# Attention steps of two heads and two key blocks, and rotary temporaries taken off the pooling chain, in a fused decoder block on eight cores

## Chip, cores, metric

One Trainium2 chip, all 8 NeuronCores, each with two of the 16 sequences (4096 tokens). The metric is the time of the slowest core, in microseconds (us), as the median of several executions. "Before" was 1694 us (1692 to 1696, 3 runs).

Executions come in two states. In the slow state the cores of one or both dies show a lower granted TensorE clock and the run is some per cent longer. One core has TensorE (PE), with its weight loads shown apart (PEld), VectorE (DVE), ScalarE (ACT), GpSimd (POOL) and the sync queue (SP), which here issues only DMAs.

## The reference, cut to what matters

```python
h   = x + concat[ MLA(n), POOL(n) ] @ w_out        # n = rmsnorm(x)
h   = h + relu(rmsnorm(h) @ w_up)**2 @ w_down
out = rmsnorm(h)

# MLA: latents c_q (384), c_kv (256), shared rotary key k_rope (64); 4 heads of 128 + 64 rotary
s = einsum(q, k) * scale                  # causal
o = softmax(s) @ v
# POOL: 4 channel groups, trailing means over 2, 4, 8, 16 tokens, minus the token itself
pooled = (cs - lo) / cnt - x
```

SEQ is 2048, D_MODEL 1024, D_FF 4096. Everything is float32 at the interface; the kernel's matmuls run in bf16.

## The kernel before

A tile is 512 tokens; a core has 8 tiles, four per sequence. Attention of tile t is one long loop over head pairs and key blocks. Into it the kernel weaves "filler" chunks: the output projection of tile t-1 (W), then all input projections of tile t+1 (P), then the transposes for tile t+2 (N). The feed-forward part comes after all eight tiles.

PSUM has 8 banks of 128x512 float32. During attention, three are fixed (two output accumulators, one for the row sums), and five rotate first-in first-out among the scores and the filler:

```python
bank = deque(range(8)); OB = (5, 6); RB = 7        # 5, 6, 7 leave the queue when attention begins
def acquire(): return bank.popleft()
def release(k): bank.append(k)
```

One attention step before: one key block j, two heads a. The rotary part of the score has 64 rows, the rest 128.

```python
def emit_S(i):
    pr, j = steps[i]
    ks = [acquire(), acquire()]
    for a, k in enumerate(ks):
        r = slice(64 * a, 64 * a + 64)
        mm(pm[k], kpe[sl][r, o:o + P], qpe[qs][r, pr, q0:T], True, False, ...)      # 64-row shape
    for a, k in enumerate(ks):
        mm(pm[k], knT[sl][:, h, o:o + P], qn[qs][:, h, q0:T], False, True, ...)     # full shape
    for k in ks:
        act(pT[p], pm[k], AF.Exp, ...); release(k)
        # diagonal blocks: masked by VectorE
# per step: emit_S(i + 1); filler; then P.V of step i (full), and after every second j
# four row-sum matmuls (32-column shape)
```

The pooled sums run on POOL, as one chain over the four groups with two temporaries, sA and sB. The rotary query of the second head pair uses the same two:

```python
def u_group(g):
    k = win_mm(768 + g * P, "win_b")
    act(u[:, 16:16 + T], pm[k], AF.Copy, ...)                       # the chain starts here
    for l in range(1, g + 2):
        dst = sA if l % 2 == 1 else sB
        tt("pool", dst[...], src[...], src[...], ALU.add, ...)
    # ... scale, subtract, write the pooled half of mixT

def q_rope(pr):
    tmp = (rstd[:, 0, :], rstd[:, 1, :]) if pr == 0 else (sA[:, 0:T], sB[:, 0:T])
    for w in range(2):
        # 3 matmuls into a bank
        tt("dve", tmp[w], pm[k], cs[:, w, :], ALU.mult, ...)
    tt("dve", qpe[qs][:, pr, :], tmp[0], tmp[1], ALU.add, ...)
```

The output projection needs x again. It has two buffers for four row blocks, so the load of block 2 waits until the store of block 0 has landed:

```python
def f(b, nh, part):                                   # W, row block b
    # 8 matmuls
    tt("dve", d, pm[k], d, ALU.add, ...)              # d: half of xr[b % 2]
    if nh == 1:
        dma("sp", rows(out_d, t, b), xr[b % 2], ...)  # store
        if b + 2 < 4: ld(b + 2)                       # load x into the same buffer
```

And POOL's queue also issues the conversion of the feed-forward weights from float32 to bf16, HBM to HBM, in 16 pieces. They depend on nothing, so they go out when POOL is through with the chain that stands ahead of them in its queue (at 217.3 us in the timeline below):

```python
STAGE = [...]                                          # 8 pieces of w_up, 8 of w_down
def stage(n):
    for _ in range(min(n, len(STAGE))):
        dma("pool", o, i, (), [r])
# "g": two calls inside P, one inside the next tile's W
```

The softmax here doesn't subtract the row's maximum and nothing guards it: scores larger than these inputs give would overflow.

## Time and profile before

The profile records one execution. First, of the kernel before, the head of its page: the span and PE's busy time with its share.

```profile
span 1682.4 us, 23203 instructions; the slowest of 8 cores (1672.6 to 1682.4 us)
## 1 busy us (share of the span) xinstructions
PE 1503.3 (89%) x7484; PEld 661.2 (39%) x7484; DVE 581.9 (35%) x873; ACT 597.4 (36%) x1147; POOL 366.1 (22%) x387
```

The table of stretches for the kernel before, on its slowest core: attention, then feed-forward (the start is left out). Columns are length, busy time of PE, weight loads, VectorE, ScalarE and POOL with counts, granted clock, DMA share, GB/s.

```profile
78.30:765.00 686.70, 554.87 (x2922) 223.90 (x2922) 262.27 (x454) 320.07 (x629) 191.06 (x207) 0.92 0.48 112
765.00:1682.40 917.40, 909.84 (x4373) 418.78 (x4373) 275.16 (x352) 239.29 (x454) 141.59 (x128) 1.00 0.13 48
```

PE fills the feed-forward stretch (910 of 917 us). In the attention stretch it is idle for 132 of 687 us. Why is in the list of waits of the kernel before (who <- for whom: us in total, times, longest). L323 is the matmul helper, L332 the two-operand elementwise helper; "arena" is all of SBUF, so the names say little and the engines much.

```profile
PE pm L323 <- DVE arena L332: 134.8, 32, 14.2
DVE arena L332 <- DMA arena<-x: 83.5, 11, 14.7
DVE arena L332 <- POOL arena L332: 82.7, 8, 14.1
PE pm L323 <- ACT arena L329: 2.1, 5, 0.5
```

PE waits for VectorE, and VectorE for two things: eight times (once per tile) for POOL, and for loads of x. Both can be seen in one tile's timeline (kernel before, end of tile 1 and start of tile 2; start, length, engine, line, operation, and in brackets the idle time before it and what ended it):

```profile
204.34 1.62 PE L323 MATMUL pm<-arena 128*128 128x512 bf16 x10
...
216.13 1.26 POOL L332 TENSOR_TENSOR arena<-arena 128x512 bf16<-128x512 f32 x1
217.33 1.57 POOL L353 DMA_DIRECT2D wup_bf<-w_mlp_up  x3
217.49 1.29 DVE L332 TENSOR_TENSOR arena<-pm,arena 128x512 f32<-128x512 f32 x2 [12.89 <-POOL arena L332]
218.33 0.59 PE L323 MATMUL pm<-arena 64*128 64x128 bf16 x3 [12.37 <-DVE arena L332]
...
218.92 0.33 SPq L353 DMA_DIRECT2D arena<-cs_tab  x1
...
239.23 0.36 SPq L353 DMA_DIRECT2D out<-arena  x1
...
253.85 0.35 SPq L353 DMA_DIRECT2D arena<-x  x1
...
258.44 0.69 DVE L332 TENSOR_TENSOR arena<-pm,arena 128x512 f32<-128x512 f32 x1 [14.66 <-DMA arena<-x]
259.27 1.12 PE L323 MATMUL pm<-arena 64*128 64x512 bf16 x2 [8.85 <-DVE arena L332]
```

At 217.3 POOL ends its chain. VectorE, which has waited 12.9 us for sA, goes on, and so does PE. At the same moment POOL issues three weight conversions, and 1.6 us later the loads of the cosine table (cs_tab) follow, which had waited for VectorE. At 239.2 the store of row block 0 goes out; the load that waits for it is issued only at 253.9, 14.6 us later (a store's median is 3.1 us), and PE stands another 8.9 us.

What a change of shape costs PE can be read from the start times of its matmuls: 216 ns from one full 128x512 matmul to the next, 312 ns from a full one to a 64-row pair, 319 ns from the pair back to a full one. So each change costs about 0.1 us.

### The profile page before, as it was taken

What the parts mean: (1) busy time and instruction counts of PE and PEld (TensorE: products, weight loads), DVE (VectorE), ACT (ScalarE), POOL (GpSimd) and SP (SyncE); (2) the same over time, 40 slices, a digit from 0 to 9 for tenths busy, and PEclk for the clock granted to TensorE, in tenths of its full rate; (3) what the DMA queues carried; (4) which work ended last, traced back from release to release, by engine and by line L of the source; (5) the groups of instructions that cost most, each with busy time, mean ns of one, the idle gap of its engine ahead of it and who ended that gap; (6) DMA issues with size and microseconds to landing.
All of it is one profiled execution on the core that took longest, in us unless ns stands there. A gap on an engine that the chain in (4) does not pass through costs nothing.

```text
span 1682.4 us, 23203 instructions; the slowest of 8 cores (1672.6 to 1682.4 us)
## 1 busy us (share of the span) xinstructions
PE 1503.3 (89%) x7484; PEld 661.2 (39%) x7484; DVE 581.9 (35%) x873; ACT 597.4 (36%) x1147; POOL 366.1 (22%) x387
## 2 busy tenths in 40 slices
PE   5567878788867879799999999999999999999998
PEld 2223333333322333233444444444444444444443
DVE  5543524314352524233332331333323313333222
ACT  6354535445332535462224123232241232322312
POOL 1650411406060513301111111110121112101210
PEclk9799988999988989999999999999999999999999
DMA  9344272643837171375402011020020110200001
GB/s 297 103 133 109 99 100 72 128 108 88 150 88 129 47 125 64 139 224 173 165 26 76 0 51 51 1 101 1 23 79 0 49 53 1 101 1 19 32 1 51
DMA packets 36133, 137.08 MB, mean 81 GB/s; under 512 B 4272, under 2 KB 4272, under 8 KB 35120
## 3 DMA queue, kind: packets, MB, share of 16 engines
q1 hardware_dynamic: 31616, 105.66, 18.8%
q0 software_dynamic: 4064, 29.36, 10.5%
q8 instruction: 64, 1.05, 0.3%
q10 hardware_dynamic: 336, 0.57, 0.1%
q14 instruction: 53, 0.43, 0.1%
HBM read 118.28 MB, written 51.38 MB: 101 GB/s over the span
## 4 chain that ended last, share of the span: by engine, by line
PE 75%; POOL 11%; DMA 6%; ACT 3%; issue 3%; DVE 2%; POOLq 0%; DVEq 0%; ACTq 0%; SPq 0%
PE pm L323 73%; POOL arena L332 8%; DMA out<-arena 4%; POOL arena L338 3%; ACT arena L329 2%; DMA arena<-x 2%; PE pm L326 2%; DVE arena L332 1%; POOL arena L347 1%; DVE arena L341 0%; DVE arena L347 0%; POOL arena L353 0%; ACT arena L390 0%; POOLq L125 0%; DVEq L125 0%
## 5 line engine op out<-in xcount | busy, mean ns | idle before, releaser
L323 PE MATMUL pm<-arena 128*128 128x512 bf16 (+3 forms) x6968 | 1472.1, 379 | 141.1 <-DVE arena L332 134.8
L323 PEld LDWEIGHTS pm<-arena 128*128 128x128 bf16 (+3 forms) x6968 | 626.2, 98 | 972.4 <-issue 303.0
L329 ACT ACTIVATE arena<-pm 128x512 bf16<-128x512 f32 (+4 forms) x768 | 412.0, 569 | 845.8 <-PE pm L323 770.6
L332 POOL TENSOR_TENSOR arena<-arena 128x512 bf16<-128x512 f32 (+6 forms) x248 | 280.6, 1131 | 776.1 <-ACT arena L329 755.6
L332 DVE TENSOR_TENSOR arena<-pm,arena 128x512 f32<-128x512 f32 (+2 forms) x288 | 197.5, 690 | 594.4 <-PE pm L323 372.4
L332 DVE TENSOR_TENSOR arena<-arena 128x512 bf16<-128x512 f32 (+3 forms) x355 | 195.0, 564 | 385.7 <-ACT arena L329 382.9
L329 ACT ACTIVATE arena<-arena 128x1 f32<-128x1 f32 (+5 forms) x200 | 104.6, 530 | 209.9 <-DVE arena L332 191.0
L335 DVE SCALAR_TENSOR_TENSOR arena<-arena 128x1024 bf16<-128x1024 f32 (+1 forms) x64 | 82.6, 1319 | 66.5 <-ACT arena L329 66.5
L347 POOL COPY arena<-arena 128x16 f32<-128x16 f32 x48 | 14.6, 304 | 338.0 <-ACT arena L329 338.0
L390 ACT ACTIVATE arena<-arena 128x1024 bf16<-128x1024 f32 x64 | 67.7, 1057 | 16.5 <-DMA arena<-out 11.6
L326 PE MATMUL pm<-arena 128*128 128x128 bf16 x516 | 41.0, 236 | 30.5 <-DVE arena L341 27.4
L326 PEld LDWEIGHTS pm<-arena 128*128 128x128 bf16 x516 | 36.1, 107 | 40.8 <-issue 35.5
L338 POOL TENSOR_SCALAR arena<-arena 128x512 f32<-128x512 f32 x32 | 49.0, 1530 | 2.6 <-POOL arena L332 1.3
L347 DVE COPY arena<-pm 128x1024 bf16<-128x1024 bf16 (+1 forms) x65 | 42.2, 681 | 18.5 <-PE pm L326 18.4
L341 DVE TENSOR_SCALAR arena<-arena 128x1024 bf16<-128x1024 f32 (+4 forms) x48 | 43.2, 912 | 12.4 <-ACT arena L329 7.4
L347 DVE CAST arena<-pm 128x512 bf16<-128x512 f32 x40 | 25.6, 685 | 17.0 <-PE pm L323 16.9
L350 POOL MEMSET arena<- 128x16 f32 (+3 forms) x15 | 2.4, 172 | 71.0 <-ACT arena L329 70.6
L353 POOL DMA_DIRECT2D arena<-wup_bf x8 | 5.7, 707 | 50.0 <-DMA arena<-wup_bf 50.0
L390 ACT ACTIVATION_READ_ACCUMULATOR arena<-arena 128x1 f32 x64 | 12.5, 195 | 0.0
L353 POOL DMA_DIRECT2D arena<-arena x8 | 4.7, 590 | 35.7 <-ACT arena L329 35.7
L329 ACT ACTIVATE arena<-pm,arena 128x512 f32<-128x512 f32 x16 | 10.9, 680 | 1.0 <-PE pm L323 0.9
L329 ACT ACTIVATION_READ_ACCUMULATOR arena<-arena 128x1 f32 x32 | 6.0, 186 | 0.0
(17 smaller groups left out, 22.9 us busy)
## 6 DMA issues: line engine op xcount, KB each, us to landing
arena<-x SPq DMA_DIRECT2D x64, 512.0 KB, 4.6
out<-arena SPq DMA_DIRECT2D x64, 512.0 KB, 3.1
arena<-out SPq DMA_DIRECT2D x28, 512.0 KB, 5.7
wup_bf<-w_mlp_up POOLq DMA_DIRECT2D x8, 1024.0 KB, 18.8
wdn_bf<-w_mlp_down POOLq DMA_DIRECT2D x8, 1024.0 KB, 24.0
arena<-wup_bf POOLq DMA_DIRECT2D x8, 1024.0 KB, 7.6
arena<-wdn_bf SPq DMA_DIRECT2D x8, 1024.0 KB, 16.8
arena<-cs_tab SPq DMA_DIRECT2D x28, 128.0 KB, 28.3
```

Source lines behind the costliest of these rows:

```text
L323: return S.add("pe", lambda e: e.matmul(out, lhsT=lhsT, rhs=rhs, start=start, stop=stop, skip_group_check=skip), reads, writes)
L326: return S.add("pe", lambda e: e.transpose(out=out, in_=in_, identity=ident), list(reads) + ["ident"], writes)
L329: return S.add("act", lambda e: e.activation(out=out, in_=in_, func=func, **kw), reads, writes, extra=extra)
L332: return S.add(eng, lambda e: e.tensor_tensor(out=out, in0=in0, in1=in1, op=op), reads, writes, extra=extra)
L335: return S.add(eng, lambda e: e.scalar_tensor_tensor(out=out, in0=in0, scalar=scalar, in1=in1, op0=op0, op1=op1), reads, writes, extra=extra)
L338: return S.add(eng, lambda e: e.tensor_scalar(out=out, in0=in0, scalar1=s1, scalar2=s2, op0=op0, op1=op1), reads, writes)
L341: return S.add(eng, lambda e: e.tensor_scalar_mul(out, in0, s1), reads, writes)
L347: return S.add(eng, lambda e: e.tensor_copy(out=out, in_=in_), reads, writes)
L350: return S.add(eng, lambda e: e.memset(ap, val), (), writes)
L353: return S.add(eng, lambda e: e.dma_start(out=out, in_=in_), reads, writes, dma=True, extra=extra)
L390: S.add("act", lambda e: e.activation(out=ring[b % len(ring)][0], in_=xs[:, b, :], func=AF.Square, scale=1.0 / 32.0, accum_out=ss_t[:, so ...
```

## The change

Its intent: (1) steps of two key blocks, so that four 64-row, four full and four row-sum matmuls each stand together and PE changes shape less often; (2) both rotary pairs use rstd as temporary, so VectorE no longer waits for POOL; (3) the cosine load leaves W; (4) at the start, rotary angles first and weight scaling split between ScalarE and VectorE. The diff, cut to its core:

```diff
         def q_rope(pr):
-            tmp = (rstd[:, 0, :], rstd[:, 1, :]) if pr == 0 else (sA[:, 0:T], sB[:, 0:T])
-            nm = [("rstd", 0), ("rstd", 1)] if pr == 0 else ["sA", "sB"]
+            nm = [("rstd", 0), ("rstd", 1)]
...
-                tt("dve", tmp[w], pm[k], cs[:, w, :], ALU.mult, [("pm", k)] + CSN, [nm[w]])
+                tt("dve", rstd[:, w, :], pm[k], cs[:, w, :], ALU.mult, [("pm", k)] + CSN, [nm[w]])
...
-        steps = [(pr, j) for pr in range(2) for j in range(nkb)]
+        steps = [(pr, j) for pr in range(2) for j in range(0, nkb, 2)]
...
-            ks = [acquire(), acquire()]
-            for a, k in enumerate(ks):
+            bl = [(j, a, max(0, j - 4 * c) * P, acquire()) for j in (j0, j0 + 1) for a in range(2)]
+            for j, a, q0, k in bl:
                 r = slice(64 * a, 64 * a + 64)
                 mm(pm[k][:, 0:T - q0], kpe[sl][r, o:o + P], qpe[qs][r, pr, q0:T], True, False,
...   # likewise the full matmuls, the exponentials, P.V and the row sums, four at a time
-    rope_angles()
     for kc in range(8):
-        win_scale(winb_f, "win_b", 640, kc, "act")
+        win_scale(winb_f, "win_b", 640, kc, ("act", "dve")[kc % 2])
...
     for j in range(3):
-        tsm("dve", wq[:, j, 0:768], wq_f[:, j, 0:768], gq_c[:, j:j + 1], ["wq_f", "sm"], ["wq"])
         tsm("dve", halves(wq, j, 0), halves(wq_f, j, 0), gqn_t[:, j:j + 1], ["wq_f", "gqn"], ["wq"])
         tsm("dve", halves(wq, j, 1), halves(wq_f, j, 1), gq_c[:, j:j + 1], ["wq_f", "sm"], ["wq"])
+        act(wq[:, j, 0:768], wq_f[:, j, 0:768], AF.Copy, ["wq_f", "sm"], ["wq"], scale=gq_c[:, j:j + 1])
...
+    P_chunks(1)["cs"][1]()
...   # cut: position loads on the sync queue, the cosine chunk moved behind the transposes
```

More of the change, by code (lines that the diff above doesn't have):

```diff
@@ L360, in build_program @@
     for q in range(4):
-        dma("act", posi[q * 32:(q + 1) * 32, :], pos_d[q * D:(q + 1) * D].partition_broadcast(32), (), [("posi", q)])
+        dma("sp", posi[q * 32:(q + 1) * 32, :], pos_d[q * D:(q + 1) * D].partition_broadcast(32), (), [("posi", q)])
     for b in range(4):
@@ L538, in q_rope @@
                     mm(pm[k], wq[:, j, c0:c0 + P], sq[:, j, :], j == 0, j == 2, ["wq", ("sq", j)], [("pm", k)])
-                tt("dve", tmp[w], pm[k], cs[:, w, :], ALU.mult, [("pm", k)] + CSN, [nm[w]])
+                tt("dve", rstd[:, w, :], pm[k], cs[:, w, :], ALU.mult, [("pm", k)] + CSN, [nm[w]])
                 release(k)
-            tt("dve", qpe[qs][:, pr, :], tmp[0], tmp[1], ALU.add, nm, [("qpe", qs, pr)])
+            tt("dve", qpe[qs][:, pr, :], rstd[:, 0, :], rstd[:, 1, :], ALU.add, nm, [("qpe", qs, pr)])
         def qn_group(h):
@@ L581, in P_chunks @@
         return d
-    FLOW = ("cs c0 c1 n0 c2 n1 c3 n2 c4 n3 kr sq nr fs u3 sk s0 u2 kp s1 u1 s2 u0 g r0 q0 t0 q1 r1 t1 q2 t2 q3 t3 "
+    FLOW = ("c0 c1 n0 c2 n1 c3 n2 c4 n3 kr sq nr fs u3 sk s0 u2 kp s1 u1 s2 u0 g r0 q0 t0 q1 r1 t1 q2 t2 q3 t3 cs "
             "k0 k1 k2 k3 v0 v1 v2 v3 g").split()
@@ L660, in emit_S @@
         def emit_S(i):
-            pr, j = steps[i]
-            sl, o = (t0 + j // 4) % KVS, (j % 4) * P
-            q0 = max(0, j - 4 * c) * P
-            ks = [acquire(), acquire()]
-            for a, k in enumerate(ks):
+            pr, j0 = steps[i]
+            bl = [(j, a, max(0, j - 4 * c) * P, acquire()) for j in (j0, j0 + 1) for a in range(2)]
+            for j, a, q0, k in bl:
+                sl, o = (t0 + j // 4) % KVS, (j % 4) * P
                 r = slice(64 * a, 64 * a + 64)
@@ L668, in emit_S @@
                    [("kpe", sl), ("qpe", qs, pr)], [("pm", k)])
-            for a, k in enumerate(ks):
+            for j, a, q0, k in bl:
+                sl, o = (t0 + j // 4) % KVS, (j % 4) * P
                 h = 2 * pr + a
@@ L672, in emit_S @@
                    [("knT", sl, h), ("qn", qs, h)], [("pm", k)])
-            ps = []
-            for k in ks:
+            out = []
+            for j, a, q0, k in bl:
                 p = pti[0]
@@ L680, in emit_S @@
                     tt("dve", pT[p][:, 0:P], pT[p][:, 0:P], keep, ALU.min, [("pT", p), "keep"], [("pT", p)])
-                ps.append(p)
-            live[i] = (j, q0, sl, ps)
+                out.append((j, a, q0, (t0 + j // 4) % KVS, p))
+            live[i] = out
         def fin1():
@@ L702, in attention @@
         for i in range(n):
-            pr, j = steps[i]
+            pr, j0 = steps[i]
             if i + 1 < n:
                 emit_S(i + 1)
-            if j == 0 and pr == 1:
+            if j0 == 0 and pr == 1:
                 fill(max(total * i / n, done[0] + 6))
                 run_late()
-            fill(max(total * (i + 1) / n, done[0] + (20 if j == 0 else 0)))
-            j, q0, sl, ps = live[i]
-            for a in range(2):
+            fill(max(total * (i + 1) / n, done[0] + (22 if j0 == 0 else 0)))
+            bl = live.pop(i)
+            for j, a, q0, sl, p in bl:
                 h = 2 * pr + a
-                mm(pm[OB[a]][:, q0:T], Vc[sl][:, j % 4, h * P:(h + 1) * P], pT[ps[a]][:, 0:T - q0], j == 0, j == nkb - 1,
-                   [("V", sl, j % 4), ("pT", ps[a])], [("O", a)])
-            if j % 2 == 1:
-                for jj, qq, _, pp in (live[i - 1], live[i]):
-                    for a in range(2):
-                        if c > 0:
-                            qd, w = 64 * a + 32 * (jj % 2), 32
-                            st, sp = jj < 2, jj >= nkb - 2
-                        else:
-                            qd, w = 64 * a, 64
-                            st, sp = jj == 0, jj == nkb - 1
-                        mm(pm[RB][qd:qd + w, qq:T], ones[:, 0:w], pT[pp[a]][:, 0:T - qq], st, sp, ["ones", ("pT", pp[a])], ["R"], skip=True)
-                del live[i - 1], live[i]
-                if j + 1 == nkb:
-                    fin1()
-                    late.append(lambda pr=pr: fin2(pr))
+                mm(pm[OB[a]][:, q0:T], Vc[sl][:, j % 4, h * P:(h + 1) * P], pT[p][:, 0:T - q0], j == 0, j == nkb - 1,
+                   [("V", sl, j % 4), ("pT", p)], [("O", a)])
+            for j, a, q0, sl, p in bl:
+                if c > 0:
+                    qd, w = 64 * a + 32 * (j % 2), 32
+                    st, sp = j < 2, j >= nkb - 2
+                else:
+                    qd, w = 64 * a, 64
+                    st, sp = j == 0, j == nkb - 1
+                mm(pm[RB][qd:qd + w, q0:T], ones[:, 0:w], pT[p][:, 0:T - q0], st, sp, ["ones", ("pT", p)], ["R"], skip=True)
+            if j0 + 2 == nkb:
+                fin1()
+                late.append(lambda pr=pr: fin2(pr))
         fill(total + 1)
@@ L762, in build_program @@
     chain0 = ordered(FLOW0, p0, N_chunks(1))
+    rope_angles()
+    act(rs_t[:, 0:1], eps_t, AF.Exp, ["eps"], [("rs", 0)])
     for b in range(4):
@@ L766, in build_program @@
         norm_scale(xt, XT_N, 0, b, one=True)
-        norm_tr(b)
+        if b > 0:
+            norm_tr(b - 1)
+    norm_tr(3)
     for kc in range(8):
@@ L777, in build_program @@
     ts("dve", gqn_t, gq_c, -1.0, None, ALU.mult, ALU.bypass, ["sm"], ["gqn"])
+    halves = lambda w_, j, x_: w_[:, j, 768:1024].rearrange("p (h x f) -> p h x f", h=4, x=2)[:, :, x_, :]
+    for _, f in chain0[6:11]:
+        f()
     for j in range(2):
-        tsm("dve", wkv[:, j, :], wkv_f[:, j, :], gkv_c[:, j:j + 1], ["wkv_f", "sm"], ["wkv"])
-    for _, f in chain0[6:7]:
-        f()
-    halves = lambda w_, j, x_: w_[:, j, 768:1024].rearrange("p (h x f) -> p h x f", h=4, x=2)[:, :, x_, :]
+        act(wkv[:, j, :], wkv_f[:, j, :], AF.Copy, ["wkv_f", "sm"], ["wkv"], scale=gkv_c[:, j:j + 1])
     for j in range(3):
-        tsm("dve", wq[:, j, 0:768], wq_f[:, j, 0:768], gq_c[:, j:j + 1], ["wq_f", "sm"], ["wq"])
         tsm("dve", halves(wq, j, 0), halves(wq_f, j, 0), gqn_t[:, j:j + 1], ["wq_f", "gqn"], ["wq"])
         tsm("dve", halves(wq, j, 1), halves(wq_f, j, 1), gq_c[:, j:j + 1], ["wq_f", "sm"], ["wq"])
+        act(wq[:, j, 0:768], wq_f[:, j, 0:768], AF.Copy, ["wq_f", "sm"], ["wq"], scale=gq_c[:, j:j + 1])
     KVN = lambda s_: [("knT", s_, h) for h in range(4)] + [("kpe", s_)] + [("V", s_, b) for b in range(4)]
@@ L794, in build_program @@
     S.alias([("wop_f", 2), ("wop_f", 3)], ["wkv_f"])
-    for _, f in chain0[7:]:
+    for _, f in chain0[11:]:
         f()
+    P_chunks(1)["cs"][1]()
     ts("dve", psn_t, ps_c, -1.0, None, ALU.mult, ALU.bypass, ["sm"], ["psn"])
@@ L850, in build_program @@
             pt = P_chunks(t + 1) if t + 1 < NT else {}
-            w = W_chunks(t - 1, ordered(["cs", "c0"], pt))
+            w = W_chunks(t - 1, ordered(["c0"], pt))
             fl += w[:7] + ordered(["g"], st) + w[7:]
@@ L857, in build_program @@
                 fo["fs"] = (0, lambda: ([f() for _, f in fc[:4]], S.alias([("mixT", 1, i) for i in range(8)], [("wop_f", 2), ("wop_f", 3)])))
-            fl += ordered(FLOW if t == 0 else FLOW[2:], P_chunks(t + 1), N_chunks(t + 2) if t + 2 < NT else {}, st, fo)
+            pt = P_chunks(t + 1)
+            if t > 0:
+                del pt["c0"]
+            del pt["cs"]
+            nx = {"cs": P_chunks(t + 2)["cs"]} if t + 2 < NT else {}
+            fl += ordered(FLOW, pt, nx, N_chunks(t + 2) if t + 2 < NT else {}, st, fo)
         if t == 0:
```

## The prediction

> **What bounds the kernel now.** The profiled span is 1682 us (timed median 1694). By the table of stretches, attention with its projections (0 to 765 us) holds 593 us of PE work; the feed-forward part (765 to 1682) holds 910 us of PE work in 917 us, untouched. The first part's PE idle, by the PE timeline, is about 170 us:
>
> 1. In each of 8 tiles VectorE waits for POOL before the second rotary pair (list of waits: 82.7 us in 8 waits). Both use sA/sB, so the rotary product queues behind POOL's 27.5 us chain of pooled sums; behind VectorE, PE stands 9.8, 11.3, 12.4, 8.3, 5.1, 14.2, 12.5, 5.9 us: 79 us.
> 2. In tiles 2 to 6 PE stands again (8.9, 4.3, 7.4, 9.3, 4.3 us) at the third row block of the output projection, whose residual x must wait until the first block's store has landed (12 to 16 us; normally 3.1).
> 3. Prologue: a hole of 10.4 us behind VectorE (weight scaling ahead of the squares), 20 us of load latency.
>
> Tensor shapes: between equal full matmuls the start-to-start time is 216 ns. Full to 64-row pair is 312, pair to full 319; two such pairs in a row take 312+3+223+3+308. So a separate pair costs 0.2 us more than a joined one. The Trainium skill, "TensorEngine Tiling (Array Packing)", Key Properties, has mode changes drain the array; the trace agrees: 0.1 us each way.
>
> **What the change does.**
> - Steps of two key blocks: 160 pair visits become 80 visits of four. 80 x 0.2 = 16 us less PE time. A step now takes 4 of 5 rotating PSUM banks; four exponentials (4 x 0.57) fit under the step's 2.7 us of PE: little new waiting.
> - The rotary wait on POOL disappears; the cosine load leaves the output projection.
> - Prologue: angles first, scaling split between engines. ScalarE gets 4.6 us of weight scaling just where it must evacuate k and q: 8 us, not 20.
>
> **How much is critical.** Not the 79 us. POOL, once its chain is done, issues three weight conversions (217, 314, 414, 502, 592 us); for 30 us their packets[...] fill the DMA engines. The skill's "DMA: Bandwidth & Descriptors" (Arbitration) has engines alternate between queues by packet[...]. From the chain's start to PE's restart I read 69.5, 68.9, 68.2, 68.7, 66.6 us whatever the attention's length: a fixed POOL-plus-DMA path. Without the rotary wait PE only reaches item 2 earlier and stands there longer, 15 to 20 us. With cosine loads out of the way the path shortens to about 65 (about 58 in tile 4, whose store may beat the conversions).
>
> Sum: prologue 8, tile 0 10, switches outside the fixed paths 8, five paths 24, last tiles 10: 60.
>
> **Predicted 1634 us (3.5% faster), range 1595 to 1662.** Chances: over 2% faster 0.87, within 2% 0.12, slower 0.01.
>
> **In the profile:** 64-row visits in fours; no VectorE wait on POOL; waits at the output projection's x loads grow to 15-20 us per tile in tiles 2 to 6; chain-start-to-restart near 65 us; feed-forward unchanged near 917 us.
>
> **What would make it wrong.** If the store lands before the conversions start, the full 79+16+20 us appear (about 1580). If four-bank steps make PE wait for exponentials, or the prologue's ScalarE load shows, less (about 1660).

## The result, and the profile after

The changed kernel took 1673 us (fast runs 1672.2, 1672.8 and 1673.1; one slow run). Its ratio to before is 0.9874, with a 95% interval of 0.9851 to 0.9896: 1.3% faster, where 3.5% was predicted, and outside the predicted range. All ratios here are the mean time of one kernel's fast runs over that of the other's in the same rounds, on the same chip, so not quite the ratio of the medians quoted.

The page and the stretches of the changed kernel:

```profile
span 1671.5 us, 23128 instructions; the slowest of 8 cores (1641.5 to 1671.5 us)
PE 1502.4 (90%) x7484; PEld 664.9 (40%) x7484; DVE 577.3 (35%) x872; ACT 592.7 (35%) x1149; POOL 370.5 (22%) x387
```

```profile
79.10:753.30 674.20, 548.21 (x2923) 226.41 (x2921) 258.96 (x454) 313.40 (x629) 195.93 (x207) 0.91 0.51 115
753.30:1671.50 918.20, 911.01 (x4373) 419.06 (x4373) 273.14 (x352) 239.46 (x454) 142.78 (x128) 0.99 0.13 48
```

The feed-forward stretch is as it was; PE's idle time in the attention stretch is 126 us against 132. The waits of the changed kernel:

```profile
DVE arena L332 <- DMA arena<-x: 105.7, 7, 26.2
PE pm L323 <- DVE arena L332: 101.4, 22, 23.0
PE pm L323 <- DVE arena L347: 17.8, 11, 3.8
PE pm L323 <- ACT arena L329: 16.0, 15, 4.6
```

The wait of VectorE on POOL, 82.7 us before, is gone from the list. The wait on loads of x has grown from 83.5 to 105.7 us, and two waits of PE that were 3 and 2 us are now 18 and 16: on L347, VectorE's copies out of PSUM, and on ScalarE. The same tile's timeline in the changed kernel:

```profile
204.93 1.73 SPq L353 DMA_DIRECT2D arena<-cs_tab  x4
...
207.00 13.31 PE L323 MATMUL pm<-arena 128*128 128x512 bf16 x63
...
213.90 1.56 POOL L353 DMA_DIRECT2D wup_bf<-w_mlp_up  x3
...
221.13 15.22 PE L323 MATMUL pm<-arena 128*128 128x512 bf16 x80 [0.83 <-DVE arena L332]
...
223.66 0.34 SPq L353 DMA_DIRECT2D out<-arena  x1
...
246.86 0.33 SPq L353 DMA_DIRECT2D arena<-x  x1
...
251.10 0.69 DVE L332 TENSOR_TENSOR arena<-pm,arena 128x512 f32<-128x512 f32 x1 [21.77 <-DMA arena<-x]
251.94 2.51 PE L323 MATMUL pm<-arena 64*128 64x384 bf16 x6 [15.58 <-DVE arena L332]
```

PE now runs through where it stood for 12.4 us. It sends the store at 223.7 in place of 239.2, but the store's landing is waited for over 23.2 us, and PE stands 15.6 us in place of 8.9. The three conversions go out at nearly the same time in both. The DMA packets of the two traces show what the load of x waits for: the last of the conversions' packets ends at 249.8 us before and at 245.6 changed, and the load follows at 253.9 and 246.9. After such a stall PE pays once more: the full matmuls of the changed kernel start 427 ns apart until 257.2 us, where the profile shows a granted clock of 0.5, and 216 ns apart after that.

The whole picture, as medians over the eight cores, from the traces' start times. A "chain" is POOL's chain of pooled sums, a "path" runs from its start to PE's restart after the stall at the output projection of the next tile; there are five of them (chains 3 to 7). "Rotary only" is experiment e3 below.

| us | before | changed | rotary only |
|---|---|---|---|
| attention begins | 77.7 | 78.8 | 71.2 |
| 2nd chain starts | 100.8 | 107.4 | 94.8 |
| 3rd chain starts | 188.8 | 186.3 | 174.1 |
| sum of five paths | 338.4 | 328.7 | 315.2 |
| in them: conversions, issue to last packet | 146.4 | 154.4 | 142.3 |
| in them: last packet to the load of x | 25.6 | 5.9 | 7.1 |
| PE stall inside them | 28.4 | 73.9 | 68.2 |
| sum of the five stretches between | 124.6 | 134.6 | 127.0 |
| 8th chain starts | 650.3 | 650.4 | 617.1 |
| attention ends | 759.4 | 745.0 | 717.6 |
| span | 1680.7 | 1665.4 | 1637.8 |

### The profile page after: what moved, and what is told of

Its sections match the earlier page's. It is cut to its first block, busy times and chain, and to the rows that moved or that the text cites. A ratio compares the mean times of both kernels' runs of the same rounds, so it can differ in the third digit from the quotient of the medians.

```text
span 1671.5 us, 23128 instructions; the slowest of 8 cores (1641.5 to 1671.5 us)
## 1 busy us (share of the span) xinstructions
PE 1502.4 (90%) x7484; PEld 664.9 (40%) x7484; DVE 577.3 (35%) x872; ACT 592.7 (35%) x1149; POOL 370.5 (22%) x387
## 4 chain that ended last, share of the span: by engine, by line
PE 80%; DMA 10%; DVE 4%; ACT 3%; issue 2%; POOL 1%; SPq 0%; DVEq 0%; ACTq 0%; POOLq 0%
PE pm L323 79%; DMA out<-arena 7%; ACT arena L329 3%; DVE arena L332 2%; PE pm L326 1%; DMA arena<-x 1%; DVE arena L341 1%; DMA arena<-cs_tab 1%; DVE arena L347 1%; DMA arena<-wout 1%; POOL arena L332 0%; ACT arena L390 0%; DMA arena<-positions 0%; SPq L353 0%; DVE arena L335 0%
## 5 line engine op out<-in xcount | busy, mean ns | idle before, releaser
L323 PE MATMUL pm<-arena 128*128 128x512 bf16 (+5 forms) x6968 | 1474.1, 380 | 137.9 <-DVE arena L332 101.4
L323 PEld LDWEIGHTS pm<-arena 128*128 128x128 bf16 (+3 forms) x6968 | 632.9, 99 | 965.9 <-issue 291.6
L329 ACT ACTIVATE arena<-pm 128x512 bf16<-128x512 f32 (+4 forms) x768 | 406.5, 573 | 828.8 <-PE pm L323 767.9
L332 POOL TENSOR_TENSOR arena<-arena 128x512 bf16<-128x512 f32 (+6 forms) x248 | 284.2, 1146 | 767.9 <-ACT arena L329 741.6
L332 DVE TENSOR_TENSOR arena<-arena 128x512 bf16<-128x512 f32 (+3 forms) x355 | 191.3, 554 | 416.7 <-ACT arena L329 413.6
L347 POOL COPY arena<-arena 128x16 f32<-128x16 f32 x48 | 15.5, 323 | 329.8 <-ACT arena L329 329.8
L326 PEld LDWEIGHTS pm<-arena 128*128 128x128 bf16 x516 | 33.3, 102 | 33.1 <-issue 27.4
L341 DVE TENSOR_SCALAR arena<-arena 128x1024 bf16<-128x1024 f32 (+3 forms) x47 | 43.3, 942 | 6.1 <-DMA arena<-win_b 3.4
L347 DVE COPY arena<-pm 128x1024 bf16<-128x1024 bf16 (+1 forms) x65 | 41.6, 680 | 10.4 <-PE pm L326 10.4
L347 DVE CAST arena<-pm 128x512 bf16<-128x512 f32 x40 | 25.4, 683 | 17.2 <-PE pm L323 17.1
```

The costliest lines, as they stand in the source:

```text
L323: return S.add("pe", lambda e: e.matmul(out, lhsT=lhsT, rhs=rhs, start=start, stop=stop, skip_group_check=skip), reads, writes)
L326: return S.add("pe", lambda e: e.transpose(out=out, in_=in_, identity=ident), list(reads) + ["ident"], writes)
L329: return S.add("act", lambda e: e.activation(out=out, in_=in_, func=func, **kw), reads, writes, extra=extra)
L332: return S.add(eng, lambda e: e.tensor_tensor(out=out, in0=in0, in1=in1, op=op), reads, writes, extra=extra)
L341: return S.add(eng, lambda e: e.tensor_scalar_mul(out, in0, s1), reads, writes)
L347: return S.add(eng, lambda e: e.tensor_copy(out=out, in_=in_), reads, writes)
```

## The experiments

The theories. **A**: a fixed path (chain, conversions, store, load of x) sets the length of tiles 1 to 6 and took in the gain of the rotary fix. **B**: the steps, which take four of the five rotating banks, cost PE about what the rotary fix gains. **C**: the reworked start lost what it should have won. Seventeen runs were made, of fifteen kernels (e16 and e17 repeat e13 and e11), on five chips; all results were right. "Fast" is the median of fast runs, "n" their number; kernels marked with the same letter shared a chip and the runs of before.

| run | kernel | chip | fast, us (n) | ratio to before, interval |
|---|---|---|---|---|
| - | changed kernel | - | 1672.8 (3) | 0.987, 0.985 to 0.990 |
| e1 | changed, conversions gated | p | 1583.0 (3) | 0.935, 0.933 to 0.938 |
| e2 | before, conversions gated | p | 1647.5 (2) | no interval |
| e3 | before + rotary temporaries | p | 1645.5 (3) | 0.970, 0.968 to 0.973 |
| e4 | before + steps | p | 1697.7 (3) | 1.003, 1.000 to 1.006 |
| e5 | rotary + gate | q | 1560.5 (4) | 0.919, 0.915 to 0.924 |
| e6 | rotary + gate + steps | q | 1575.1 (4) | 0.928, 0.924 to 0.932 |
| e7 | changed, old steps | q | 1660.6 (2) | 0.978, 0.972 to 0.985 |
| e8 | changed, start mended | q | 1664.1 (4) | 0.980, 0.976 to 0.984 |
| e9 | e8 + old steps + gate | r | 1567.5 (4) | 0.922, 0.918 to 0.925 |
| e10 | e5 with 4 rotating banks | r | 1568.8 (3) | 0.923, 0.918 to 0.928 |
| e11 | e6 + copies on ScalarE | r | 1554.9 (4) | 0.914, 0.911 to 0.918 |
| e12 | e5 + other start | r | 1567.3 (3) | 0.921, 0.918 to 0.925 |
| e13 | e5 + copies on ScalarE | s | 1557.1, 1572.4 | no interval |
| e14 | changed + copies on ScalarE | s | 1653.8 (2) | 0.975, 0.969 to 0.981 |
| e15 | e8 + gate + copies on ScalarE | s | 1559.7 (4) | 0.919, 0.916 to 0.923 |
| e16 | as e13 | t | 1557.2 (6) | 0.922, 0.917 to 0.927 |
| e17 | as e11 | t | 1552.5 (3) | 0.916, 0.911 to 0.921 |

### The path: e1 and e2 gate the conversions, e3 changes the temporaries alone

The gate issues three conversions at a time, only after the fourth row block of W has been added. By then all loads of x that PE will wait for have landed.

```diff
-    def stage(n):
+    def stage(n, extra=()):
...
-            dma("pool", o, i, (), [r])
+            dma("pool", o, i, (), [r], extra=extra)
...
-        st = {"g": (0, lambda: stage(1))} if t > 0 else {}
+        st = {}
...
-            fl += w[:7] + ordered(["g"], st) + w[7:]
+            fl += w + [(0, lambda: stage(3, extra=[S.lastw[("xr", 1)]]))]
```

e1, this edit in the changed kernel:

> The changed kernel, with the weight conversions issued in threes only once the fourth row block of the output projection has been added, instead of at the end of POOL's chain. Theory A (the path chain of pooled sums, conversions, store, x load sets the length of tiles 1 to 6, and took in the gain): the stalls at the output projection (15.6, 11.3, 17.3, 23.0, 13.0 us in the changed kernel) nearly vanish, and the time falls by 50 to 75 us to 1600 to 1625 us. Theory B (steps that take four of five PSUM banks cost what the rotary fix gains): PE waits elsewhere instead, on ScalarE and PSUM, and the time falls by at most 20 us, to 1655 or more. Result right.

Measured: 1583 us, 90 us less than the changed kernel and below even theory A's range. The timeline of e1 in the same tile:

```profile
222.13 0.34 SPq L353 DMA_DIRECT2D out<-arena  x1
224.92 0.33 SPq L353 DMA_DIRECT2D arena<-x  x1
...
240.45 1.57 POOL L353 DMA_DIRECT2D wup_bf<-w_mlp_up  x3 [27.74 <-DVE arena L332]
```

The store goes out at the same time as in the changed kernel (222.1 against 223.7), but the load of x follows 2.8 us later in place of 23.2, and the conversions come when nothing waits for the DMA engines. The spread of the cores also shrinks, from 30 us (1641.5 to 1671.5) to 7 (1574.4 to 1581.0), but the median core gains 88 us, too, so the spread is not what makes e1 beat its range. Part of the rest is slow matmuls, as after the stall shown above. What full matmuls at about twice their usual distance lost during attention is, as median over the cores, 21 us in the changed kernel and 11 in e1 (before 17, e2 12; e3 16, e5 6). No expectation had this term, and e1, e2 and e5 all came out below their ranges. Theory A is confirmed for the changed kernel.

e2, the same edit in the kernel before:

> The kernel before, with the same gate on the conversions. Theory A: the five stalls at the output projection (34 us in all) vanish, the eight rotary waits (79 us) stay and now count in full: 1655 to 1670 us. So the changed kernel gated beats this by 45 us or more, while ungated it beats its own by only 21. Theory B: the two gated kernels differ by about the same 20 us as the ungated. Result right.

Measured: 1645.3 and 1649.6 us in its two fast runs, 46 us below before (1693.8 on that chip), more than the 34 us of stalls expected: it undershot the range by 8 us. The rotary waits stayed. Gated, the changed kernel beats before by 64 us (1647.5 - 1583.0), ungated by 21: as A says, the conversions hid most of it.

e3, only `q_rope` from the diff:

> The kernel before with only the rotary temporaries changed; steps, prologue and conversions as before. Theory A: the rotary waits vanish, the stalls at the output projection grow by nearly as much in tiles 2 to 6; only tiles 0, 6 to 7 and a little of the rest gain: 1665 to 1680 us. Theory B: the whole gain shows once the four-bank steps are away: 1650 us or less.

Measured: 1645.5 us, a ratio of 0.970. That is 20 us below the lower end for A and within theory B. This part of the change, alone, gains more than twice what all of it gains. Its five paths fell by 23 us (338.4 to 315.2), and its stalls grew to 68 us: A's mechanism is there, too. So both theories hold in part, and the rest of the change costs about 27 us. But the path is not as fixed as theory A has it. The sync queue of e3 in the same tile (core 1):

```profile
189.49 2.31 SPq L353 DMA_DIRECT2D arena<-cs_tab  x4
209.19 0.36 SPq L353 DMA_DIRECT2D out<-arena  x1
233.87 0.35 SPq L353 DMA_DIRECT2D arena<-x  x1
```

The cosine loads still stand in W here, but go out 11.7 us ahead of the conversions (201.2), since VectorE no longer waits for POOL; before, they went out behind them and ahead of the store on the same queue. In the tile shown of before, none of the store's packets starts until 250.2. From the last conversion packet to the load of x the five paths take 7.1 us in e3, 25.6 before.

### The steps: e4 to e7 and e10

e4, the kernel before with the attention steps alone:

> The kernel before with only the attention steps of two key blocks. Theory A: 80 pair visits of 0.2 us go, most of that under the fixed path: 1685 to 1695 us, the five stalls a little longer. Theory B: slower than before, 1700 us or more, with PE waits on ScalarE (PSUM) that before does not have.

Measured: 1697.7 us, ratio 1.003. No gain at all; nearer to B, though too little to decide by itself.

e5 (temporaries and gate) and e6 (the same with the steps) take the fixed path away, so that nothing hides the steps' worth:

> The kernel before with the rotary temporaries changed and the conversions gated; old steps, old start. Of the run with the temporaries alone (1646 us) the five stalls (19.5, 8.6, 12.7, 19.2, 12.1 us) should vanish: 1575 to 1595 us, so the temporaries alone give 60 to 80 us once the conversions are out of the way, against 49 with them in the way. Result right.

> The same with the steps of two key blocks added. With no fixed path to hide under, the 80 saved pair visits of 0.2 us should show: 8 to 16 us less than with the old steps (theory A). If the steps lose PE time to PSUM waits (theory B) it is the same or slower than with the old steps. Result right.

Measured: 1560.5 us for e5, 15 us below its range, and 1575.1 us for e6. So with the stall gone the steps do not save 16 us, they cost 14.6. The traces say why. In them, summed between the first and last attention matmul, medians over the eight cores:

| us | e5, old steps | e6, new steps | e11, new steps, copies moved | e16, old steps, copies moved |
|---|---|---|---|---|
| spent in changes of shape | 39.6 | 23.6 | 23.9 | 40.0 |
| waits over 150 ns inside a run of 64-row matmuls | 1.6 | 16.3 | 14.2 | 2.3 |
| other waits over 600 ns | 29.7 | 33.1 | 22.3 | 28.3 |
| whole stretch | 564.0 | 578.2 | 557.3 | 560.4 |

The 16 us of saved shape changes are real: 39.6 to 23.6. But the run of four 64-row matmuls now stops inside itself, mostly at the fourth, which needs the fourth bank: 15 us. Behind the run PE waits for copies out of PSUM. The waits of PE on the slowest core, first e5:

```profile
PE pm L323 <- DVE arena L347: 6.6, 8, 1.2
PE pm L323 <- ACT arena L329: 1.7, 6, 0.4
```

then e6:

```profile
PE pm L323 <- DVE arena L347: 20.3, 13, 4.1
PE pm L323 <- ACT arena L329: 5.8, 17, 0.8
```

And one such wait in e6's timeline. The CAST on L347 copies the rotated key out of its bank; it stands on VectorE behind two products of 2.51 us in all and a normalisation of 1.54 us, and PE, which has used the other banks for the step, waits 3.0 us for it:

```profile
177.94 2.51 DVE L332 TENSOR_TENSOR arena<-arena 128x512 bf16<-128x512 bf16 x2 [0.42 <-ACT arena L329]
178.47 1.18 PE L323 MATMUL pm<-arena 64*128 64x384 bf16 x5 [0.47 <-ACT arena L329]
...
180.37 1.54 DVE L341 TENSOR_SCALAR arena<-arena 128x1024 bf16<-128x1024 f32 x1
181.83 0.68 DVE L347 CAST arena<-pm 128x512 bf16<-128x512 f32 x1
...
182.65 2.72 PE L323 MATMUL pm<-arena 128*128 128x512 bf16 x6 [3.00 <-DVE arena L347]
```

In the table, shape changes and waits inside the runs nearly cancel. The 14 us that e6 is longer are mostly the waits on copies outside the runs (from 7 to 16 us, mean over the cores; some 4 us of the copies' waits are inside the runs and already in the 15) and the slow full matmuls after waits (from 6 to 13 us).

The Trainium skill, "TensorEngine Tiling (Array Packing)", Gotcha 1, says that row tiling raises PSUM pressure and that different row tiles write to different banks. Here a pair of 64-row tiles takes two banks and two pairs in one run take four; the trace agrees with 15 us of waits inside the runs.

e7, the changed kernel with the old steps:

> The changed kernel with the attention steps of before; its start and cosine loads kept, conversions not gated. If the steps cost PE its lead over the stalled store (10 to 15 matmuls fewer done before each stall, 2 to 3 us in each of five tiles, and less at the first chain's start), the time falls by 10 to 15 us from 1673 to about 1660. If the loss is all in the start, it stays at 1670 or more. Result right.

Measured: 1659.3 and 1661.8 us in two fast runs (two more were slow), 12 us below the changed kernel, as expected. In its one profile the five paths took 315.2 us, as in e3, and not 328.7, and the stretches between took 127.3 us and not 134.6. On six of the eight cores (the others lack some records), PE does 46 fewer full matmuls inside the paths in the changed kernel (819 against 865 of before) and 46 more in the stretches between (523 against 477); 46 times 0.216 is 9.9 us moved from where PE has time to where it has none. With the new steps PE gets less far ahead before it stalls. This fits the longer stretches. The longer path it does not explain: of the 13 us, 12 to 14 are the conversions themselves, 154.4 us from issue to last packet in the changed kernel, 142.3 in e3 and 140.8 in e7. The cores of the changed kernel's profile differ more than that among themselves (127 us on the fastest core, 162 on the slowest), so one profile each does not show that the steps cause it.

e10 takes a bank from e5, to see whether the number of banks matters to the old steps as well:

```diff
+    held_back = bank.pop()               # ahead of the attention of the first tile
...
     bank.extend([5, 6, 7])               # after the last one
+    bank.append(held_back)
```

> Temporaries and gate alone (1560.5 us), old steps, with four rotating PSUM banks in place of five. If the steps of two key blocks lose because they leave too few banks (theory B), taking a bank from the old steps also costs, 8 us or more: 1568 to 1590, with PE waits on VectorE and ScalarE. If bank depth is not what binds, within 4 us of 1560. Result right.

Measured: ratio 0.923 against 0.919 of e5, about 6 us, with overlapping intervals: between the two expectations, and inconclusive on its own. Its trace leans to theory B: the stretch of the table above is 7 us longer than in e5, the waits inside the 64-row runs are 6.4 us in place of 1.6, and PE's waits on ScalarE 8 in place of 2. So the number of banks matters somewhat to the old steps, too.

### Freeing banks sooner: e11, e13, e14, e16, e17

```diff
-            cp("dve", Vc[ks][:, b, :], pm[k], [("pm", k)], [("V", ks, b)])
+            act(Vc[ks][:, b, :], pm[k], AF.Copy, [("pm", k)], [("V", ks, b)])
...
-            cp("dve", kpe[ks], pm[k], [("pm", k)], [("kpe", ks)])
+            act(kpe[ks], pm[k], AF.Copy, [("pm", k)], [("kpe", ks)])
```

> Temporaries, gate and new steps (1575 us), with the PSUM copies of v and of the rotated key on ScalarE in place of VectorE, where they wait behind other work and hold a bank (PE waits of 3.2 us each in tiles 1, 2 and 5, 20 us in all on those copies). If held banks are what the steps lose by, 8 to 15 us come back: 1560 to 1567. If it is ScalarE itself that is late, no gain: 1573 or more. Result right.

Measured: ratio 0.914 against 0.928 of e6, about 23 us (20 between the medians, across chips), more than expected. The waits of PE in e11:

```profile
PE pm L323 <- ACT arena L329: 5.8, 12, 1.8
PE pm L323 <- DVE arena L347: 3.9, 4, 1.3
```

The waits on L347 are gone (20.3 to 3.9 us) and those on ScalarE did not grow. But the waits inside the 64-row runs hardly shrank (16.3 to 14.2 us in the table above); the gain lies in the waits behind the runs. So held banks explain the part on L347. Most of the part inside the runs is waits for ScalarE (8.4 us in e6, 9.0 in e11, mean over the cores) and stays; that these are its exponentials, and the depth of the rotation, was not tested. The slow full matmuls after waits fell from 13 to 6 us.

The control, the same move with the old steps:

> Control for the copies on ScalarE: temporaries, gate and those copies with the OLD steps. If the copies cost the new steps alone because these need four banks, the move gives little here: ratio to before 0.914 to 0.921 (0.919 without the move), and the new steps with the move (0.914) are level or ahead. If the move helps any kernel by the same 23 us, the ratio is about 0.906 and the new steps are still the slower ones. Result right.

Measured: 1557.1 and 1572.4 us; no interval, and two more runs were slow. So it was run once more, beside the new steps on one chip in five rounds:

> Temporaries, gate, copies on ScalarE, OLD steps. The undisturbed cores of the control spanned 1547 to 1556 us: ratio to before 0.915 to 0.919. Result right.

> The same with the NEW steps. If the 16 us of saved shape changes are real and what is left of bank waits eats most of them: 2 to 10 us below the old steps on the same chip, ratio 0.911 to 0.915. If the steps are worth nothing: level or slower. Result right.

Measured: 0.922 (0.917 to 0.927) for the old steps, 0.916 (0.911 to 0.921) for the new; medians 1557.2 and 1552.5 us. Six of e17's nine runs were slow, so it rests on three. The ratios narrowly missed both expectations (0.915 to 0.919 and 0.911 to 0.915). Two of e16's six fast runs (1573 and 1578 us) show two cores at a lower clock, much as three of e17's slow runs do (1578 to 1580 us), and just pass as fast; without these two, the old steps stand at 0.918 and the gap is 4 us. The move of the copies is worth about 3 us with the old steps (medians of e5 and e16, across chips) and over 20 with the new. With it the steps go from a loss of 15 us to a gain of about 5, a third of the shape changes they save. That they are ahead at all is likely and not certain: the intervals overlap.

e14 makes the move in the changed kernel itself:

> The changed kernel with the copies of v and of the rotated key on ScalarE; conversions not gated. If held banks are what the steps lose by here too: up to 10 us less (ratio 0.980 to 0.985 against 0.987), no more, since the stalls at the output projection take in what is won before them. If nothing of it shows: 0.987. Result right.

Measured: 1653.6 and 1654.0 us, ratio 0.975, 19 us below the changed kernel. The expectation, at most 10, was wrong: I held that the stalls would take it in. In its trace the five paths fell from 328.7 to 316.4 us. PE sends the store 14 us sooner there after the conversions' issue (39.5 in place of 53.5 us over the five paths), but then waits as long for it (107.0 us in both). The path is shorter because the conversions took 137.6 us in place of 154.4. Why is not shown. The matmuls inside the paths are about as few as in the changed kernel (817 and 819), so their count is not what lengthens the path.

### The start: e8, e9, e12 and e15

Two waits in the changed start were not in the old one. The timeline of the changed kernel, at the scaling of the query weight and at the first use of the output weight:

```profile
53.29 0.94 ACT L329 ACTIVATE arena<-arena 128x768 bf16<-128x768 f32 x1 [3.19 <-DVE arena L341]
...
54.34 2.42 DVE L341 TENSOR_SCALAR arena<-arena 128x128 bf16<-128x128 f32 x2 [1.14 <-ACT arena L329]
...
56.85 0.94 ACT L329 ACTIVATE arena<-arena 128x768 bf16<-128x768 f32 x1 [2.62 <-DVE arena L341]
...
102.55 1.15 ACT L329 ACTIVATE arena<-arena 128x1024 bf16<-128x1024 f32 x1 [3.55 <-DMA arena<-wout]
```

ScalarE and VectorE take turns. They write different columns of the query weight, but the kernel's dependency tracker knows it under one name, so each write waits for the one before. And the loads of the output weights wait for everything that touched the cosine tile, which now includes the second cosine load. The edit of e8:

```diff
-        tsm("dve", halves(wq, j, 0), ..., ["wq"])            # and halves(wq, j, 1)
+        tsm("dve", halves(wq, j, 0), ..., [("wq", 1)])
-        act(wq[:, j, 0:768], ..., ["wq"], ...)
+        act(wq[:, j, 0:768], ..., [("wq", 0)], ...)
...
-    P_chunks(1)["cs"][1]()
     ts("dve", psn_t, ps_c, -1.0, None, ALU.mult, ALU.bypass, ["sm"], ["psn"])
     ex = S.deps_of(WF + ["cosv", "wkv_f"] + CSN)
+    P_chunks(1)["cs"][1]()
```

> The changed kernel with two false waits of its start taken away: the query weight's parts under names of their own (VectorE and ScalarE waited for each other three times between 51.9 and 60.2 us), and the load of the output weights no longer waiting for the second cosine load (ScalarE waited 4.1 us for it at 99 to 104 us). 7 to 14 us less than 1673: 1659 to 1666. If only the steps matter: 1670 or more. Result right.

Measured: 1664.1 us, 9 us less, as expected. Attention begins at 71.9 us in place of 78.8 and the second chain at 98.7 in place of 107.4.

e9 puts e8's start, the gate and the old attention steps together.

> The changed kernel with the old attention steps, the mended start (query weight parts named apart, output weights not behind the cosine load) and the gated conversions. Against the run with temporaries and gate alone (1560.5 us): the mended start began attention at 72 us, as that run did, so if the start and the cosine move are worth nothing more it is equal within 5 us (1555 to 1566); with the steps it was about 1575. Result right.

Measured: ratio 0.922 against 0.919 of e5: equal within 5 us. So the reworked start, even mended, is worth nothing over the old one once the rotary wait is gone; the old start with the new temporaries begins attention at 71 us, too (e3). What it removed was the same wait.

e12 keeps e5's scaling and only reorders its start: a part of tile 0's first chunks goes ahead of the scaling of the latent weights, and the query weights are scaled later (the lines stand for loops).

```diff
+    chunks 6 to 10 of tile 0
-    chunk 6 of tile 0
-    scale wq                             # VectorE
     scale wkv
+    chunks 11 to 18 of tile 0
+    scale wq                             # VectorE
-    chunks 7 and on of tile 0
+    chunks 19 and on of tile 0
```

> Temporaries and gate alone (1560.5 us), with the start of the kernel before reordered on VectorE: the squares and normalised latents ahead of the kv weight scaling, the query weight scaling only after the first keys and values. The hole of PE at 40 to 51 us should shrink by 4 us: 1555 to 1559. If PE waits for something else there, no change. Result right.

A miss: 0.921 against 0.919, no gain. The hole at 40 us stayed (11.3 us on one core, still behind VectorE), and a second one of 6.3 us came up where the query weights were scaled later.

e15 is e8 with the gate and with the copies on ScalarE.

> The changed kernel with everything mended: copies on ScalarE, gate, query weight parts named apart, output weights not behind the cosine load. The new steps, temporaries, gate and copies on the old start gave 0.914; the mended start alone began attention at the same 72 us. So equal to that within 0.5%: 0.910 to 0.919. Result right.

Measured: 0.919 (0.916 to 0.923), at the end of the range and a little behind e11 (0.914). The fastest measured is a simple mix (the intervals of e11, e15, e16 and e17 overlap): the kernel before with the rotary temporaries, the gate, the new steps and the copies on ScalarE (e11 and e17), at 1553 to 1555 us, 8.5% below before and 7% below the changed kernel.

## Why the prediction was wrong

It predicted 1634 us (1595 to 1662); measured was 1673. Point by point, with the eight-core medians of the table:

- **The rotary wait and the path: right in mechanism, though the path is not fixed.** The wait on POOL disappeared; the stalls at the output projection grew to 15.6, 11.3, 17.3, 23.0 and 13.0 us on the slowest core ("15 to 20 us"). For the temporaries alone the five paths shrank by 23 us (e3), where the prediction put 24. This is in part luck: the prediction gave the 24 to the moved cosine loads, and e3 does not move them. The rotary fix itself sent them out ahead of the conversions, and the wait after the last conversion packet fell by 18.5 us. e1 showed that it is the conversions that hold the path. The packets with data have 32 KB and took 4.5 us (median, the tile shown of before), and in the changed kernel the load of x follows 1 us after the last of them (5.9 us over the five paths).
- **"80 x 0.2 = 16 us less PE time ... little new waiting": the step that failed.** The first half was right to the microsecond (39.6 to 23.6 us of shape changes). The second was not. I compared average loads, four exponentials of 0.57 us against 2.7 us of PE, and did not ask who else holds the one bank that is left over. The runs showed 15 us of waits inside the four-matmul runs, 9 more of PE on VectorE's copies outside them, and 7 of slow matmuls after waits (e6 against e5). The steps cost 12 us in the changed kernel (e7), where the sum had a gain of 8.
- **The five paths, 24 us: given back.** In the whole change they gained 10 (338.4 to 328.7): the wait after the last conversion packet fell by 20, and the conversions took 8 longer and the chains 4. The stretches between lost 10 (124.6 to 134.6), 7 of them with the steps (e7). The sum from the third chain to the eighth is 461.5 us before and 464.1 after.
- **Prologue, 8 us: measured -1.** Of the risk that I named (ScalarE's weight scaling) the larger part was a false dependency under one name, worth 7 us at the start of attention (e8). **Tile 0, 10 us**: up to the third chain start and tile 0 together gained 2.5 us (188.8 to 186.3). Without the false dependency and the output weights' wait for the cosine load it is 9 (e8).
- **Last tiles, 10 us: measured 14.5** (from the eighth chain to the end of attention, 109.1 to 94.6), where no conversion is in the way.
- Feed-forward unchanged: right (917 and 918 us).

Of the 27 us between the temporaries alone and the whole change, the steps account for 12 (e7) and the start for 9 (e8), if the two add up. Some 6 us stay open. So does why, with the new steps and the copies on VectorE, the path got longer by 13 us (e3 to the changed kernel): the conversions took 12 us longer there and not with the copies moved (e14), in one profile each, but no run shows a link from banks to conversions.

## What to carry to other kernels

Before costing a wait that a change removes, follow what the freed engine meets next: here a DMA path, started by an engine off the critical path, set the tile's length, and moving its start by a few lines was worth more than the whole change. When a step claims more of a shared buffer pool, ask how long each other user holds its share, not whether the average loads fit. And after splitting one buffer's work between engines, split its name in the dependency tracker, too.

## What the Trainium skill lacked or had wrong

- "TensorEngine Tiling (Array Packing)", Key Properties, says that changing the tiling mode drains the array, but gives no cost: here 92 to 106 ns per change (full to 64-row 96, 64-row to full 92 to 103, full to 32-column 93, 32-column to 64-row 106), about 40 us in all over the attention of e5.
- The same page, Gotcha 1, names PSUM pressure from row tiling without a number: with four of five rotating banks per step it cost more (15 us inside the runs, 9 on copies outside them) than the 16 us of shape changes it saved.
- "DMA: Bandwidth & Descriptors", Queues, rings and completion order (Arbitration), has engines alternate between queues by packet. The traces fit that roughly: in the tile shown of before, three conversions are 96 packets of 32 KB that took 3.4 to 5.5 us each, and from 228 us on 16 to 32 packets of the sync queue's loads started with every 16 of them. But the page doesn't say what this means for a small transfer beside a converting one from HBM to HBM: a 512 KB store with a median of 3 us was waited for over 12 to 16 us before, and over 23 us in the tile shown of the changed kernel, until the conversions were through.
- No page speaks of the spread between cores that such transfers can bring: 30 us between the fastest and the slowest core of the changed kernel (10 us before), where the conversions of the five paths took 162 us on the slowest core and 127 on the fastest; 7 us with them gated (e1).
